# A hybrid decoder block on one core: another source for one Strassen-Winograd product, hand-fixed places for the input squares, and another order in the last value product

## The chip, the cores and the metric

The kernel runs on one core of a Trainium2 chip. The metric is the device time of one execution in microseconds; less is better. The engines of the core work side by side: TensorE (PE in the profile, its weight loads PEld), VectorE (DVE), ScalarE (ACT), GpSimd (POOL) and SyncE (SP), which issues the DMAs. Each engine takes its instructions in a fixed order.

## The reference

One block on x of 1024 tokens by 1024 channels, all in float32:

```python
xn = rmsnorm(h, norm_mix_g)
proj = xn @ w_in                                   # q, k, v (512 each), u, vg (512 each), 8 gates
log_f = log_sigmoid(proj[..., G_END:] + b_forget)
att = forgetting_attention(q, k, v, log_f)         # causal, 8 heads of 64, decay from cumsum(log_f)
u, vg = split(gelu(proj[..., V_END:G_END]))
sg = u * (tril(w_s) @ rmsnorm(vg) + b_s)           # in chunks of 128 tokens, 8 groups of 64
h = h + concat(att, sg) @ w_out
h = h + conv_ffn(rmsnorm(h, norm_ffn_g), ...)      # up 1024 -> 2*2816, causal conv of 3, silu gate, down
return rmsnorm(h, norm_final_g)
```

## The kernel before

**Products.** Every large product is a Strassen-Winograd product: the operands are cut in two by two blocks and seven products of blocks take the place of eight. Blocks of x transposed are `B11`, `B21` (first 512 tokens), and sums of blocks are `T1` to `T4` and `B22`, with the tokens' second half in them. Each operand is split into a rounded high part and a low part that is the rest; a block product is then three TensorE passes (high by high, high by low, low by high). ScalarE writes the high part (`act.copy`, or `activation` with the gain), VectorE the low part. `own` does so for one 128-row slice with the gain, `hl_of` for two slices whose gain is applied already, `tsplit` for a slice of weights, into a ring of six buffers. `tmul` issues the passes of one slice k for four token tiles, k by k: 12 matmuls, 48 for a product.

**Order.** A framework's scheduler puts each engine's instructions in order by its own estimates of when they are ready, earlier program text first among those that are. Two wrappers narrow this: while `act.on` and `dve.on` are true, every ScalarE and every VectorE call that goes through `act` and `dve` is tied behind the one before it on that engine; once they are false, later calls may be ordered freely, but each stays behind the last one of the hand-written stretch. Calls through `nc.scalar` are not bound, SyncE's and TensorE's neither. Because the wrappers make the calls, most ScalarE, VectorE and POOL rows show L51 (behind the previous one) or L44 (behind the floor) in place of the source line. Tiles with one tag share that tag's buffers, so a write can wait for the last reader of an older tile.

**First stage (0 to about 100 us).** The gating projections u and vg are made from seven products: B11, B21, then T2, T3, T1, T4 and B22; between B21 and T2 stand the low half of the values (`values_low`). The hand-written order covers this stretch up to T3's weights. The raw blocks of x sit in buffers that the split sets take over later: raw `x22` lies in tags x1, x2, where T3's split is to be written, and raw `x12` in tags t3, t2, where B22's is. `t2_of` has left a copy of x22 with its gain in `tmp[j][2]`. T3 = x12 g - x22 g is made in that copy. The squares of x for the first norm, one ScalarE instruction for each of 8 token tiles with `accum_out`, read `xq`, two halves in turn, so a load waits for the square two before; they stand as `nc.scalar`, outside the fixed order. `keep` evicts the kept low half of the values from PSUM and stores it to DRAM (`vd`). Behind the fixed stretch VectorE takes T2's result into `ut[1]`, adds weight blocks (`gb`), and makes T1's low parts.

**Keys and queries (about 100 to 188 us).** Four steps of products, with the forget gates in between: Exp, then Ln on ScalarE, each with a table load.

**Values and gating (188 to 224 us).** The second half of the heads' values comes from four products: T3 and B22 into four banks' halves `VH`, B11 and B21 into `VL`; two token tiles share a PSUM bank. `evac_v` evicts a tile: ScalarE's high part, VectorE's low part. `spatial` then goes through 8 groups, fixed order on: three matmuls into one of four banks, VectorE's product for the first half of the tokens, ScalarE's `second` for the other half, which GpSimd multiplies. The evictions of the value tiles 4 to 7 stand among the first groups, and a small Exp ahead of them loads the table that attention needs. `turn_sg` transposes the result for the output product, `sg_hi` and `sg_lo` split it, and attention's first logits take the PSUM banks over. Then follow attention (224 to about 500 us), the up products with the convolution, and the down products.

Of the kernel before, what the change touches and what calls it, by code (L numbers as in the profile page):

```python
# [65 lines left out]
def block_kernel(ctx: ExitStack, tc: tile.TileContext, xT, xtok, wuv, wv0, wv1, wqk, cpk, bfv,  # L66
# [37 lines left out]
    def f32(ap):  # L104
        return ap.bitcast(F32)
# [67 lines left out]
    def xset(tags):  # L173
        return [sb(t, [P, 2, 2, 512], F32R) for t in tags]
# [11 lines left out]
    def gk(k):  # L186
        return g1[:, k:k + 1]

    def xr(n, k):
        return RAW[n][k // 2][:, k % 2, :]  # L190
# [15 lines left out]
    def own(n, src, k, row):  # L206

        act.activation(xs(n, 0, k), src, AF.Copy, scale=gk(row))
        dve.scalar_tensor_tensor(out=xs(n, 1, k), in0=src, scalar=gk(row), in1=f32(xs(n, 0, k)),
                                 op0=ALU.mult, op1=ALU.subtract)  # L210

    def hl_of(n, j, src):
        act.copy(x2(n, 0, j), src)
        dve.tensor_tensor(out=x2(n, 1, j), in0=src, in1=f32(x2(n, 0, j)), op=ALU.subtract)
# [31 lines left out]
    def tsplit(src, gate=None, n=512, tag=None):  # L246
        w = sb(tag, [P, 2, n], F32R) if tag else ring(n=n)
        d = split_w(src, (w[:, 0], w[:, 1]))
        if gate:
            behind(d, gate)  # L250
        return w

    def tmul(banks, w, n, k, first, apart=False, ms_=range(4), own=True):

        ops = [(m, c) for m in ms_ for c in range(3)]
        for m, c in sorted(ops, key=lambda o: (o[1] > 0, o)) if apart else ops:
            ms = slice(m * P, (m + 1) * P)
            xi, wi = ((0, 0), (0, 1), (1, 0))[c]
            pe.matmul(banks[m], xs(n, xi, k)[:, ms], w[:, wi, :], start=(first and k == 0 and c == 0 and (own or m % 2 == 0)),  # L259
                      stop=(k == 3 and c == 2), skip_group_check=True)  # L260
# [30 lines left out]
    def keep(banks, hf):  # L291
        t = ring(F32).rearrange("p a (b c) -> p (a b) c", c=256)
        for m in range(4):
            act.copy(t[:, m, :], banks[m][:, 0:256])
            act.copy(zf[:, 4 * hf + m, 0:8], banks[m][:, 256:264])
        sp.dma_start(out=vd[hf], in_=t)
# [18 lines left out]
    values_low(3)  # L315

    xq = sb("A", [P, 2, 1024])
    for tt in range(8):
        t = xq[:, tt % 2, :]
        sp.dma_start(out=t, in_=xtok[tt * P:(tt + 1) * P, :])  # L320
        nc.scalar.activation(t, t, AF.Square, accum_out=ss1[:, tt:tt + 1])

    s2 = []

    def sum23(k):
        a11, a21, a22 = ua[k][:, 0, :], gb[k][:, 0, :], gb[k][:, 1, :]
        s2.append(sb("gg", [P, 512]))
        dve.tensor_tensor(out=a11, in0=a21, in1=a11, op=ALU.add)
        dve.tensor_tensor(out=s2[k], in0=a11, in1=a22, op=ALU.add)
# [4 lines left out]

    sum23(0)
    sum23(1)
    tmul(S, tsplit(s2[0]), "T2", 0, True)
    tmul(S, tsplit(s2[1]), "T2", 1, True)
    for k in (2, 3):
        sum4(k - 2)  # L340
        sum23(k)
    for k in (2, 3):
        tmul(S, tsplit(s2[k]), "T2", k, True)
    keep(B, 0)
    B, S = S, B
    for k in range(4):
        t3 = tmp[k // 2][2][:, k % 2]
        dve.scalar_tensor_tensor(out=t3, in0=xr("x12", k), scalar=gk(k), in1=t3, op0=ALU.mult, op1=ALU.subtract)
    XS["B22"] = xset(("t3", "t2"))
    for k in range(4):  # L350
        own("B22", xr("x22", k), k, 4 + k)
    XS["T3"] = xset(("x1", "x2"))
    for j in range(2):
        hl_of("T3", j, tmp[j][2])
        for k in (2 * j, 2 * j + 1):
            tmul(S, tsplit(ua[k][:, 0, :]), "T3", k, True)
    act.on = dve.on = False
    for m in range(4):
        dve.tensor_tensor(out=ut[1][:, m, :], in0=B[m], in1=vgt[0][:, m, :], op=ALU.subtract)
# [153 lines left out]
    def forget_sums(c, r):  # L513
        bfb, z, e = c[:, 136:144], c[:, 144:208], c[:, 208:272]
        tri, ones, lh, ll = r[:, 0:P], r[:, P:2 * P], r[:, 256:320], r[:, 320:384]
        v3 = lambda t: t.rearrange("p (h t) -> p h t", h=8)
        dve.tensor_tensor(out=v3(z), in0=zf[:, :, 0:8].rearrange("p t h -> p h t"),
                          in1=rstd1.unsqueeze(1).to_broadcast((P, 8, 8)), op=ALU.mult)
        dve.tensor_tensor(out=v3(z), in0=v3(z), in1=bfb.unsqueeze(2).to_broadcast((P, 8, 8)), op=ALU.add)
        dve.scalar_tensor_tensor(out=e, in0=z, scalar=-1.0, in1=z, op0=ALU.mult, op1=ALU.max)  # L520
        act.activation(e, e, AF.Exp, scale=-1.0)
        act.activation(e, e, AF.Ln, bias=one[:, 0:1])
        dve.tensor_scalar(out=z, in0=z, scalar1=-1.0, scalar2=0.0, op0=ALU.mult, op1=ALU.max)
        dve.tensor_tensor(out=z, in0=z, in1=e, op=ALU.add)
        dve.tensor_copy(lh, z)
        dve.tensor_tensor(out=ll, in0=z, in1=f32(lh), op=ALU.subtract)
        yield
        ps = bank()
        for o, m in ((64, tri), (128, ones)):
            pe.matmul(ps[:, o:o + 64], m, lh, start=True, stop=False)  # L530
            pe.matmul(ps[:, o:o + 64], m, ll, start=False, stop=True)
        whole, run = v3(ps[:, 128:192]), v3(e)
        dve.memset(run[:, :, 0:1], 0.0)
        for tt in range(1, 8):
            dve.tensor_tensor(out=run[:, :, tt:tt + 1], in0=run[:, :, tt - 1:tt], in1=whole[:, :, tt - 1:tt], op=ALU.add)
        dve.tensor_tensor(out=v3(z), in0=v3(ps[:, 64:128]), in1=run, op=ALU.add)

        yield
        pe.transpose(ps[0:64, 192:320], z, ident)
        rows = c[0:64, 272:400]  # L540
        act.activation(rows, ps[0:64, 192:320], AF.Copy, scale=-1.0)
        sp.dma_start(out=ncr.rearrange("h (t p) -> (h t) p", p=P), in_=rows)
        yield
# [118 lines left out]
    def evac_v(tt, hf, ps):  # L662
        v = V[tt // 2][:, tt % 2, 4 * hf:4 * hf + 4]
        p3 = ps.rearrange("p (h d) -> p h d", h=4)
        x = act.activation(v[:, :, 0, :], p3, AF.Copy, scale=rstd1[:, tt:tt + 1])
        dve.scalar_tensor_tensor(out=v[:, :, 1, :], in0=p3, scalar=rstd1[:, tt:tt + 1],
                                 in1=f32(v[:, :, 0, :]), op0=ALU.mult, op1=ALU.subtract)
        return x

    def kept(hf):  # L670
        t = sb("G" if hf else "wy", [P, 4, 256])
        sp.dma_start(out=t, in_=vd[hf])
        for j in range(4):
            if j % 2 == 0:
                V.append(sb("V", [P, 2, 8, 2, 64], F32R))
            x = evac_v(4 * hf + j, 0, t[:, j, :])
        return x

    kept(0)
# [38 lines left out]
    def spatial():  # L718

        act.on = dve.on = True  # L720
        after(tc, act.activation(pad[:, 0:1], eps, AF.Exp), stored)
        evac_v(4, 1, VH[0])
        tmp = [sb("pt", [P, 4, 256]) for _ in range(2)]
        for g in range(8):
            c, j = g // 2, g % 2
            ps = bank()
            pe.matmul(ps, ws[0][:, g, :], vgs[c][:, 0, j], start=True, stop=False)
            pe.matmul(ps, ws[0][:, g, :], vgs[c][:, 1, j], start=False, stop=False)
            m = pe.matmul(ps, ws[1][:, g, :], vgs[c][:, 0, j], start=False, stop=True)
            v3 = lambda t: t.rearrange("p (t d) -> p t d", d=64)  # L730
            u = [ut[hf][:, :, g * 64:(g + 1) * 64] for hf in range(2)]
            dve.scalar_tensor_tensor(out=u[0], in0=v3(ps[:, 0:256]), scalar=bs[:, g:g + 1], in1=u[0],
                                     op0=ALU.add, op1=ALU.mult)
            t = tmp[g // 4][:, g % 4, :]

            def second():
                act.activation(t, ps[:, 256:512], AF.Identity, bias=bs[:, g:g + 1])
                x = pool.tensor_tensor(out=u[1], in0=v3(t), in1=u[1], op=ALU.mult)
                after(tc, x, splits[0])

            if g < 7:
                second()
            if g < 3:
                evac_v(5 + g, 1, VH[1 + g])
        seq(m)
        return second

# [28 lines left out]
    S = [sbank() for _ in range(4)]  # L776

    def vbank(tt):
        return S[(2, 3, 0, 1)[tt // 2]][:, tt % 2 * 256:tt % 2 * 256 + 256]

    VH, VL = [vbank(4 + m) for m in range(4)], [vbank(m) for m in range(4)]
    a1 = [w0[k][:, :, 0:256] for k in range(4)]
# [28 lines left out]
    head_loads(0)  # L811
    for k in range(4):
        tmul(VL, w0[k][:, :, 256:512], "B21", k, False)
    stored = kept(1)
    ws = spatial_weights()
    for m in range(4):
        evac_v(m, 1, VL[m])
    for k in range(4):
        tmul(VH, tsplit(wvr[k][:, 1, :], n=256, tag="whl"), "B22", k, False)
    whs, wrs = [], sg_load(0)  # L820
    for s in range(2):
        after(tc, sp.dma_start(out=ncd[s].rearrange("h (t p) -> (h t) p", p=P), in_=sums[1 + s]), queued[0])
# [836 lines left out]
```

## Time and profile before

| | us |
|---|---|
| median of 3 runs | 1069.79 (1067.95 to 1070.84) |
| the profiled execution | 1069.69 |
| its span, first to last instruction | 1068.0 |
| TensorE busy | 1050.6 (98%) |
| VectorE busy | 887.0 (83%) |
| ScalarE busy | 571.9 (54%) |
| GpSimd busy | 236.5 (22%) |
| mean granted TensorE clock | 0.996 |

Busy time of TensorE is from modelled ends of pipelined matmuls, so a product that runs at half clock counts as busy too. In a timeline a row is: start in us, length in us, engine, line, operation, tiles out<-in, shape, count; then in brackets the engine's idle time ahead of it and what ended that. SPq is SyncE's DMA issue. In the waits' view a row is: who waited, for whom, us in total, times, longest.

### The profile page before, as it was taken

What the parts mean: (1) busy time and instruction counts of PE and PEld (TensorE: products, weight loads), DVE (VectorE), ACT (ScalarE), POOL (GpSimd) and SP (SyncE); (2) the same over time, 40 slices, a digit from 0 to 9 for tenths busy, and PEclk for the clock granted to TensorE, in tenths of its full rate; (3) what the DMA queues carried; (4) which work ended last, traced back from release to release, by engine and by line L of the source; (5) the groups of instructions that cost most, each with busy time, mean ns of one, the idle gap of its engine ahead of it and who ended that gap; (6) DMA issues with size and microseconds to landing.
All of it is one profiled execution on the core that took longest, in us unless ns stands there. A gap on an engine that the chain in (4) does not pass through costs nothing.

```text
span 1068.0 us, 14617 instructions
## 1 busy us (share of the span) xinstructions
PE 1050.6 (98%) x5156; PEld 882.5 (83%) x5156; DVE 887.0 (83%) x1299; ACT 571.9 (54%) x1015; POOL 236.5 (22%) x177
## 2 busy tenths in 40 slices
PE   9899999999999999999999999999999999999997
PEld 7778888978888887887888888888888888888886
DVE  6899697767777869999999989989998866997774
ACT  6677534466676846754444445444444444554653
POOL 0004141330420740053333333333322000000000
PEclk9999999999999999999999999999999999999999
DMA  9603365747555435132235423322321899433442
GB/s 338 199 12 129 100 170 157 226 122 209 169 156 163 136 143 204 60 99 95 102 129 173 152 88 110 108 94 94 123 105 62 294 321 318 118 99 94 144 121 96
DMA packets 67184, 155.78 MB, mean 146 GB/s; under 512 B 9028, under 2 KB 9748, under 8 KB 67112
## 3 DMA queue, kind: packets, MB, share of 16 engines
q1 hardware_dynamic: 65800, 154.82, 45.0%
q8 instruction: 40, 0.66, 0.3%
q14 instruction: 32, 0.26, 0.1%
q10 hardware_dynamic: 1312, 0.04, 0.1%
HBM read 111.96 MB, written 42.87 MB: 145 GB/s over the span
## 4 chain that ended last, share of the span: by engine, by line
PE 88%; DVE 5%; DMA 3%; ACT 2%; issue 1%; SPq 0%; DVEq 0%; ACTq 0%
PE k L1509 20%; PE qc L1251 11%; PE qa L1251 11%; PE qd L1251 10%; PE qb L1251 5%; PE ps L259 4%; PE pb L259 3%; PE pb L948 3%; PE pb L929 3%; PE qa L410 2%; PE qc L410 2%; PE qd L410 2%; PE pl L889 2%; PE pl L890 2%; PE pf L973 1%; PE pf L975 1%
## 5 line engine op out<-in xcount | busy, mean ns | idle before, releaser
L1509 PE MATMUL k<-whb,wha 128*128 128x512 f32 x924 | 209.7, 389 | 0.0
L1509 PEld LDWEIGHTS k<-whb,wha 128*128 128x128 f32 x924 | 173.3, 188 | 36.2 <-DVE wha L161 0.2
L1251 PE MATMUL qc<-xT,whb 128*128 128x512 f32 x540 | 130.0, 389 | 0.4 <-DVE u L1362 0.4
L1251 PE MATMUL qa<-xB,wha 128*128 128x512 f32 x528 | 127.3, 390 | 0.0
L1251 PEld LDWEIGHTS qc<-xT,whb 128*128 128x128 f32 x540 | 101.2, 188 | 22.1 <-DVE u L1362 0.9
L1251 PEld LDWEIGHTS qa<-xB,wha 128*128 128x128 f32 x528 | 98.8, 188 | 20.8 <-DVE wha L161 0.4
L155 ACT CAST wha<-sg 128x512 fp32r<-128x512 f32 x77 | 47.8, 622 | 96.9 <-PE k L1509 84.2
L155 ACT CAST whb<-sg 128x512 fp32r<-128x512 f32 x82 | 50.5, 618 | 86.7 <-PE qc L1251 68.3
L161 DVE TENSOR_TENSOR wha<-sg,wha 128x512 fp32r<-128x512 f32 x77 | 52.8, 688 | 40.5 <-ACT wha L155 40.4
L930 ACT CAST pt<-pb 128x512 fp32r<-128x512 f32 (+1 forms) x80 | 42.2, 544 | 43.0 <-PE pb L929 34.2
L1251 PE MATMUL qd<-xB,whb 128*128 128x512 f32 x264 | 63.9, 390 | 0.0
L1251 PE MATMUL qd<-xT,whb 128*128 128x512 f32 x264 | 63.6, 389 | 0.0
L161 DVE TENSOR_TENSOR whb<-sg,whb 128x512 fp32r<-128x512 f32 x82 | 57.7, 705 | 4.4 <-ACT whb L155 4.3
L1251 PE MATMUL qb<-xT,whb 128*128 128x512 f32 x252 | 60.9, 389 | 0.0
L1138 POOL TENSOR_TENSOR sg<-raw 128x512 f32<-128x512 f32 x20 | 30.4, 1518 | 136.1 <-DVE whb L161 75.7
L931 DVE TENSOR_TENSOR pt<-pb,pt 128x512 fp32r<-128x512 f32 (+1 forms) x80 | 48.8, 635 | 12.2 <-ACT pt L930 10.9
L1251 PEld LDWEIGHTS qd<-xB,whb 128*128 128x128 f32 x264 | 49.5, 188 | 10.7 <-DVE h L1370 0.5
L1251 PEld LDWEIGHTS qd<-xT,whb 128*128 128x128 f32 x264 | 49.5, 188 | 10.3
L1251 PEld LDWEIGHTS qb<-xT,whb 128*128 128x128 f32 x252 | 47.3, 188 | 9.8
L948 PE MATMUL pb<-pt,V 128*128 128x256 f32 x320 | 52.1, 287 | 0.3 <-DVE pt L931 0.2
L1141 POOL TENSOR_TENSOR sg<-sg,raw 128x512 f32<-128x512 f32 x20 | 33.3, 1666 | 64.2 <-DVE whb L161 64.2
L1139 POOL TENSOR_TENSOR sg<-sg,raw 128x512 f32<-128x512 f32 x20 | 34.9, 1746 | 50.7 <-issue 48.8
(404 smaller groups left out, 2292.5 us busy)
## 6 DMA issues: line engine op xcount, KB each, us to landing
raw<-wup SPq DMA_DIRECT2D x44, 512.0 KB
sg<-hx SPq DMA_DIRECT2D x77, 256.0 KB
hx<-hs SPq DMA_DIRECT2D x44, 256.0 KB
hx<-ca SPq DMA_DIRECT2D x35, 256.0 KB
xT<-wdn SPq DMA_DIRECT2D x28, 256.0 KB
x<-kd SPq DMA_DIRECT2D x24, 256.0 KB
A<-xtok SPq DMA_DIRECT2D x8, 512.0 KB
raw<-wqk SPq DMA_DIRECT2D x8, 512.0 KB
```

Source lines behind the costliest of these rows:

```text
L155: act.copy(h, src)
L161: return eng.tensor_tensor(out=l, in0=src, in1=f32(h), op=ALU.subtract)
L259: pe.matmul(banks[m], xs(n, xi, k)[:, ms], w[:, wi, :], start=(first and k == 0 and c == 0 and (own or m % 2 == 0)), stop=(k == 3 and c == ...
L410: pe.matmul(ps, w[:, wi, ks], xs(n, xi, k), start=(first and c == 0), stop=(c == 11), skip_group_check=True)
L929: seq(pe.transpose(ptr[:, c:c + P], tj[jj][:, k * P:(k + 1) * P], ident))
L930: casts.append(act.copy(pt[:, 0, 0:w], ptr[:, 0:w]))
L931: los.append(dve.tensor_tensor(out=pt[:, 1, 0:w], in0=ptr[:, 0:w], in1=f32(pt[:, 0, 0:w]), op=ALU.subtract))
L948: seq(pe.matmul(po[0][:, oo:oo + n], lhs, pt[:, s, o:o + n], start=(k == 0 and s == 0), stop=(s == 1 and half)))
L1139: pool.tensor_tensor(out=s[1], in0=s[0], in1=a11, op=ALU.add)
L1141: pool.tensor_tensor(out=s[3], in0=s[1], in1=a12, op=ALU.add)
L1251: pe.matmul(ps, w[:, wi, ks], xb[:, xi, k, :], start=(first and n == 0), stop=(n == 11), skip_group_check=True)
L1509: pe.matmul(banks[bk + m], xh[:, xi, ms], wh[:, wi, :], start=(first and p_ == 0 and n == 0), stop=(p_ == NP - 1 and n == 2), skip_group_c ...
```

## The change

Four things. T3's source is written over raw `x12` rather than over the copy of x22, T3's split comes right behind it, and B22 is split from the copy (two `hl_of` rather than four `own`) at the end of the hand-written stretch. The squares get places of their own in ScalarE's fixed order, among the weight casts. The last value product takes slices 0 and 1 for all tiles and then slices 2 and 3 tile by tile, with all its weight splits ahead; three of the four late evictions stand ahead of the gating's groups, the fourth's low part behind the first group; and the banks of the tiles are numbered in order. The small Exp moves behind the forget gates' Ln.

```diff
+    def squares(*tts):
+        for tt in tts:
+            t = xq[:, tt % 2, :]
+            sp.dma_start(out=t, in_=xtok[tt * P:(tt + 1) * P, :])
+            act.activation(t, t, AF.Square, accum_out=ss1[:, tt:tt + 1])
...
     sum23(0)
     sum23(1)
+    squares(0)
     tmul(S, tsplit(s2[0]), "T2", 0, True)
     tmul(S, tsplit(s2[1]), "T2", 1, True)
+    squares(1, 2)
     for k in (2, 3):
         sum4(k - 2)
         sum23(k)
     for k in (2, 3):
         tmul(S, tsplit(s2[k]), "T2", k, True)
+        squares(*((3,) if k == 2 else ()))
     keep(B, 0)
+    squares(4)
     B, S = S, B
     for k in range(4):
-        t3 = tmp[k // 2][2][:, k % 2]
-        dve.scalar_tensor_tensor(out=t3, in0=xr("x12", k), scalar=gk(k), in1=t3, op0=ALU.mult, op1=ALU.subtract)
-    XS["B22"] = xset(("t3", "t2"))
-    for k in range(4):
-        own("B22", xr("x22", k), k, 4 + k)
+        dve.scalar_tensor_tensor(out=xr("x12", k), in0=xr("x12", k), scalar=gk(k), in1=tmp[k // 2][2][:, k % 2],
+                                 op0=ALU.mult, op1=ALU.subtract)
     XS["T3"] = xset(("x1", "x2"))
     for j in range(2):
-        hl_of("T3", j, tmp[j][2])
+        hl_of("T3", j, RAW["x12"][j])
         for k in (2 * j, 2 * j + 1):
             tmul(S, tsplit(ua[k][:, 0, :]), "T3", k, True)
+        squares(5 + j)
+    squares(7)
+    XS["B22"] = xset(("t3", "t2"))
+    for j in range(2):
+        hl_of("B22", j, tmp[j][2])
     act.on = dve.on = False
...
-        act.activation(e, e, AF.Ln, bias=one[:, 0:1])
+        x = act.activation(e, e, AF.Ln, bias=one[:, 0:1])
+        after(tc, act.activation(pad[:, 0:1], eps, AF.Exp), x)
...
         act.on = dve.on = True
-        after(tc, act.activation(pad[:, 0:1], eps, AF.Exp), stored)
-        evac_v(4, 1, VH[0])
+        for m in range(3):
+            evac_v(4 + m, 1, VH[m])()
+        vlow = evac_v(7, 1, VH[3])
...
-            if g < 3:
-                evac_v(5 + g, 1, VH[1 + g])
+            if g == 0:
+                vlow()
...
-        return S[(2, 3, 0, 1)[tt // 2]][:, tt % 2 * 256:tt % 2 * 256 + 256]
+        return S[tt // 2][:, tt % 2 * 256:tt % 2 * 256 + 256]
...
-    for k in range(4):
-        tmul(VH, tsplit(wvr[k][:, 1, :], n=256, tag="whl"), "B22", k, False)
+    a12 = [tsplit(wvr[k][:, 1, :], n=256, tag="whl") for k in range(4)]
+    for k in range(2):
+        tmul(VH, a12[k], "B22", k, False)
+    for m in range(4):
+        for k in (2, 3):
+            tmul(VH, a12[k], "B22", k, False, ms_=(m,))
```

`evac_v` now returns its VectorE part as a function that the caller runs; elsewhere it is run at once.

More of the change, by code (lines that the diff above doesn't have):

```diff
@@ L317, in block_kernel @@
     xq = sb("A", [P, 2, 1024])
[L318 to L321, printed above, removed]
+    def squares(*tts):
[3 more added lines that the diff above has]
+            act.activation(t, t, AF.Square, accum_out=ss1[:, tt:tt + 1])
     s2 = []
@@ L665, in evac_v, with low @@
         x = act.activation(v[:, :, 0, :], p3, AF.Copy, scale=rstd1[:, tt:tt + 1])
-        dve.scalar_tensor_tensor(out=v[:, :, 1, :], in0=p3, scalar=rstd1[:, tt:tt + 1],
-                                 in1=f32(v[:, :, 0, :]), op0=ALU.mult, op1=ALU.subtract)
-        return x
+        def low():
+            dve.scalar_tensor_tensor(out=v[:, :, 1, :], in0=p3, scalar=rstd1[:, tt:tt + 1],
+                                     in1=f32(v[:, :, 0, :]), op0=ALU.mult, op1=ALU.subtract)
+            return x
+        return low
     def kept(hf):
@@ L675, in kept @@
                 V.append(sb("V", [P, 2, 8, 2, 64], F32R))
-            x = evac_v(4 * hf + j, 0, t[:, j, :])
+            x = evac_v(4 * hf + j, 0, t[:, j, :])()
         return x
@@ L813, in block_kernel @@
         tmul(VL, w0[k][:, :, 256:512], "B21", k, False)
-    stored = kept(1)
+    kept(1)
     ws = spatial_weights()
     for m in range(4):
-        evac_v(m, 1, VL[m])
-    for k in range(4):
-        tmul(VH, tsplit(wvr[k][:, 1, :], n=256, tag="whl"), "B22", k, False)
+        evac_v(m, 1, VL[m])()
+    a12 = [tsplit(wvr[k][:, 1, :], n=256, tag="whl") for k in range(4)]
[4 more added lines that the diff above has]
+            tmul(VH, a12[k], "B22", k, False, ms_=(m,))
     whs, wrs = [], sg_load(0)
```

## The prediction

> **What bounds the kernel now.** I read TensorE's waits over the whole span first, then the weight loads (PEld) in order of time around the two places that the waits name, then the windows with busy time and granted clock there, and last the timelines of ScalarE, VectorE and SyncE between them. TensorE's two longest waits inside the program lie in stages that the change touches:
>
> ```profile
> PE pb L259 <- ACT whl L51: 3.2, 1, 3.2
> PE pb L727 <- ACT pt L51: 1.6, 2, 0.8
> ```
>
> The first is the third product (T3) of the gating projections. Weight loads in order of time:
>
> ```profile
> 44.38 5.40 PEld L259 LDWEIGHTS ps<-wy,H 128*128 128x128 f32 x24
> 53.40 0.19 PEld L259 LDWEIGHTS pb<-whl,x 128*128 128x128 f32 x1 [3.63 <-ACT whl L51]
> ...
> 66.94 2.68 PEld L259 LDWEIGHTS ps<-wy,H 128*128 128x128 f32 x12
> ...
> 77.82 2.23 PEld L259 LDWEIGHTS pb<-whl,V 128*128 128x128 f32 x10
> ```
>
> T2 ends its loads at 44.38 + 5.40 = 49.78. T1, with 48 matmuls, runs without a gap from 66.94 to 77.82, 10.88 us or 0.2267 each. T3 also has 48, but takes 49.78 to 66.94, 17.16 us: 6.28 are lost. The windows say how (columns: length, busy time of PE, PEld, DVE, ACT, POOL with counts, granted clock, DMA):
>
> ```profile
> 50.20:53.40 3.20, 0.00 (x1) 0.00 (x0) 1.29 (x2) 3.20 (x6) 0.00 (x0) 1.00 0.19 78
> 55.30:58.70 3.40, 3.40 (x9) 2.65 (x8) 3.15 (x5) 3.40 (x7) 0.00 (x0) 0.50 0.00 0
> 215.70:219.10 3.40, 1.76 (x7) 0.84 (x6) 2.49 (x7) 1.56 (x4) 1.30 (x3) 1.00 0.97 223
> 219.10:222.50 3.40, 3.40 (x14) 3.01 (x14) 1.45 (x4) 1.92 (x6) 2.75 (x5) 0.50 0.44 158
> ```
>
> TensorE is idle for 3.20 us and, soon after, runs 3.4 us at clock 0.50. The same happens again after a window in which it was busy 1.76 of 3.40: a gap is paid for twice, once as idle time and up to 3.4/2 = 1.7 us more as slow matmuls behind it.
>
> The second place is the spatial gating, behind the last value product:
>
> ```profile
> 205.73 5.83 PEld L259 LDWEIGHTS ps<-whl,t 128*128 128x128 f32 x48
> 211.49 0.19 PEld L727 LDWEIGHTS pb<-H,wy 128*128 128x128 f32 x1
> 212.51 0.48 DVE L51 SCALAR_TENSOR_TENSOR A<-pb,cp,A 128x256 f32<-128x256 f32 x1 [0.42 <-PE pb L729]
> 213.03 0.47 ACT L51 ACTIVATE pt<-pb,cp 128x256 f32<-128x256 f32 x1 [1.46 <-DVE A L51]
> 214.30 0.47 DVE L51 SCALAR_TENSOR_TENSOR A<-pb,cp,A 128x256 f32<-128x256 f32 x1
> 219.77 0.23 PEld L753 LDWEIGHTS ps<-ident,A 128*128 128x128 f32 x1
> 222.98 0.91 PEld L753 LDWEIGHTS pb<-ident,A 128*128 128x128 f32 x8
> 223.10 1.89 DVE L51 TENSOR_TENSOR G<-ps,G 128x512 fp32r<-128x512 f32 x3 [0.45 <-ACT G L51]
> 224.44 0.19 PEld L889 LDWEIGHTS pl<-x 128*128 128x128 f32 x1 [0.56 <-DVE G L51]
> ```
>
> Eight groups of three matmuls need 24 x 0.2267 = 5.44 us, 211.49 to 216.93; the transposes start at 219.77, 2.84 late. One group takes 214.30 - 212.51 = 1.79 us, since VectorE, ScalarE's `second`, ScalarE's eviction and VectorE's low part of it follow each other, and from the fifth group on a bank must be freed so. Then come transposes at half clock, and attention's first logits at 224.44.
>
> **The change, T3.** In the old order T3's split waits for B22's four, since it is written over their source, and all of them share ScalarE with squares that wait for loads. The rows I build the new order from:
>
> ```profile
> 36.25 0.61 ACT L51 CAST whl<-gg 128x512 fp32r<-128x512 f32 x1
> 38.14 1.06 ACT L321 ACTIVATE A<-A 128x1024 f32<-128x1024 f32 x1 [1.29 <-DMA A<-xtok]
> ...
> 43.62 1.07 ACT L321 ACTIVATE A<-A 128x1024 f32<-128x1024 f32 x1 [0.64 <-DMA A<-xtok]
> ...
> 45.05 0.40 ACT L51 COPY whl<-pb 128x256 f32<-128x256 f32 x1
> ...
> 45.37 0.76 ACT L51 ACTIVATE t<-x,g 128x512 fp32r<-128x512 f32 x1
> ...
> 50.14 1.06 ACT L321 ACTIVATE A<-A 128x1024 f32<-128x1024 f32 x1 [1.55 <-DMA A<-xtok]
> ...
> 51.81 1.03 ACT L51 CAST x<-pt 128x1024 fp32r<-128x1024 f32 x1
> ```
>
> ```profile
> 39.32 0.33 SPq L320 DMA_DIRECT2D A<-xtok  x1
> ```
>
> ```profile
> 44.80 0.33 SPq L320 DMA_DIRECT2D A<-xtok  x1
> ```
>
> A square's load is issued when the square two before it is done, and it feeds ScalarE 43.62 - 39.32 = 4.3 us later (50.14 - 44.80 = 5.3 beside the store of `vd`). With fixed places, square 1 goes behind the cast of 36.25 and ends near 37.3; square 2 stays at 38.14; square 3's load, issued at 37.4, lands at 41.7, so square 3 ends at 42.8. Then the last T2 cast (to 43.3), eight copies of `keep` (four pairs at 45.37 - 45.05 = 0.32: 44.6), square 4 (45.7), T3's first cast, 1.03 (46.7), and two weight casts at 0.55 to 0.6 (47.8). VectorE:
>
> ```profile
> 43.02 1.41 DVE L51 SCALAR_TENSOR_TENSOR pt<-t,g,pt 128x512 f32<-128x512 f32 x2
> ...
> 52.87 1.23 DVE L51 TENSOR_TENSOR x<-pt,x 128x1024 fp32r<-128x1024 f32 x1 [0.18 <-ACT x L51]
> ...
> 54.01 0.68 DVE L51 TENSOR_TENSOR whl<-raw,whl 128x512 fp32r<-128x512 f32 x1
> ...
> 58.24 2.48 DVE L44 TENSOR_TENSOR A<-ps,G 128x512 f32<-128x512 f32 x4
> ...
> 65.81 0.65 DVE L44 TENSOR_TENSOR wy<-G,wy 128x512 fp32r<-128x512 f32 x1
> ```
>
> Its low part of the last T2 weights ends at 44.0, four in-place sums (0.7 each) end at 46.7, T3's low at 47.9, the first weights' low at 48.6. TensorE wants them at 49.78: 1.2 us to spare. The second half (cast behind square 5, low done near 51.8) is wanted 24 matmuls later, at 55.2. So T3 runs dense and ends at 49.78 + 10.88 = 60.66.
>
> What is late next is T1. B22's split now stands last in the hand-written order, behind square 7, and every later VectorE instruction is made to follow its second low part. Square 5 ends at 48.8 and square 7's load lands 3.7 to 5.3 later, at 52.5 to 54.2. Square 7, two casts of 1.03 and the last low of 1.23 put the end of the hand-written order at 56.6 (if no square waits for its load) to 58.8; I take 57.4, a load of 4.0, since by then only one other transfer is under way. Before, that point was 58.24. Behind it nothing of VectorE's work has changed: four `ut` differences, four weight sums, four T1 lows, the reciprocal, the first weights' low, 58.24 to 66.46, 8.22 us. So all of T1 but its first matmul starts at 57.4 + 8.3 = 65.7: TensorE waits 5 us there in place of 3.2 in T3. A window of low use again brings half clock: slow from the restart to the next window's edge, and one window more where the restart's own window was used less than half. Over the places where the edge can fall that costs 0.9 to 2.4 us, mean 1.6. T1 ends at 65.7 + 47 x 0.2267 + 1.6 = 77.9 against 77.82: **+0.1**, range -1.0 to +1.6. T3's 6.28 come back as a wait and slow matmuls one product later. From there TensorE has its old slack, its rows being dense to the value products.
>
> The window at 215.70 shows that half use is enough for the slow clock. The Trainium skill ("TensorE: Matmul & The Clock Gate", Part 1) says that the clock falls after one idle window of about 3.4 us; by that rule a 5 us gap holds a whole window only in some 45% of runs, the mean is 0.6 rather than 1.6, and the sum below would be 1.0 us less. The measured window speaks for the higher price.
>
> **The last value product and the gating.** Its 48 matmuls stay 5.76 us, 205.73 to 211.49. Tile by tile, the first bank (two tiles) is complete near 210.5, the second at 211.9. With hops of 213.03 - 212.51 = 0.52: the evictions of the first bank run from 210.5 to 212.4, the third tile's from 211.9 to 212.9, the first group's VectorE step at 212.9, `second` at 213.4, the fourth low behind it; the next groups follow at 0.4 to 0.5 rather than 1.79. The fifth group wants its bank at 214.2 and gets it at 213.9; the sixth 214.9 for 214.9. So the gating is dense: transposes at 216.93, no low window, full clock. The four sgT lows (the last three in the row of 223.10, 0.63 each) then set attention's start: four transposes and the cast behind them put the first low at 218.3, the second at 219.2, and the third is done at 220.5, against 224.4 before: **-3.85**. Bounds: -4.8 (TensorE alone: 24 transposes at 0.91/8 end at 219.65) and -2.0 (each of the four steps a hop late). The new bank numbers free the banks of the first transposes earlier; that costs nothing.
>
> **The table load.** It leaves this place and goes behind the keys' logarithm:
>
> ```profile
> 116.50 1.65 ACT L44 CAST whl<-raw 128x512 fp32r<-128x512 f32 x3
> 124.56 0.62 ACT L44 CAST G<-G 128x512 fp32r<-128x512 f32 x1 [6.41 <-DVE G L44]
> ...
> 209.17 1.28 ACT L51 ACT_TABLE_LOAD   x1
> ...
> 211.09 0.48 ACT L51 ACTIVATE V<-ps,rstd 128x256 fp32r<-128x256 f32 x1 [0.42 <-PE ps L259]
> ```
>
> At 209.17 it was hidden: ScalarE then still waited 0.42 for TensorE. At 116.5 it delays three casts by 1.5 us, in front of 6.4 us of idle time: 0. Without that cover it would cost 1.5.
>
> **Sum.** +0.1 - 3.85 = -3.75. The profiled execution took 1069.69 (span 1068.0, 1.69 around it), 0.1 under the median of 1069.79, so the forecast is **1065.9 us**. Its own ends are -1.0 - 4.8 = -5.8 and +1.6 - 2.0 = -0.4: 1063.9 to 1069.3. About 0.3%, 3.2 us, is what a measurement of this kernel can tell from no change.
>
> **The rivals.**
>
> *T1 is not held up* (10%). VectorE might do the `ut` differences and weight sums in its pause between 51.8 and 55. Its work from 44.0 on is 2.7 (sums) + 2.4 (T3) + 2.5 (weights) + 2.4 (B22) + 8.2 = 18.2 us, so T1 could start at 62.2 with no slow clock and end at 72.9: -4.9 - 3.85, 1060.9. Against it speaks the code: behind the hand-written order each call is tied to the last one in it.
>
> *The clock stays up behind a 5 us gap* (8%). If only a wholly idle window lowers it, T1's gap costs 1.0 less: 1064.9. This is the rule of the Trainium skill's page named above. The window that was busy 1.76 of 3.40 speaks against it.
>
> *Attention's start is held by a load* (10%). DMA was 0.97 busy at 215.70 to 219.10, and before, the first logits came only at 224.44. Had the first head's last load landed near there, the gating's 3.85 would turn into a DMA wait: 1069.69 + 0.1 = 1069.8. For it speaks the full DMA; against it, that the wait of 224.44 was for VectorE.
>
> *The squares block the split: slower* (10%). Square 4's load now stands behind the store of `vd` in the program. Rows of SyncE in the old order:
>
> ```profile
> 45.47 0.33 SPq L296 DMA_DIRECT2D vd<-whl  x1
> 47.38 0.33 SPq L320 DMA_DIRECT2D A<-xtok  x1
> ```
>
> There the store stands behind all eight loads in the program, yet goes out ahead of the last: the scheduler issues what it expects ready first, which is why I let square 4's load pass the store. If it doesn't, the load goes out at 45.1, lands 5.3 later at 50.4, and square 4, ahead of T3's first cast on ScalarE, ends at 51.5 rather than 45.7. T3's first weights are ready at 54.4 (4.7 us of idle TensorE), the order ends near 63.0, T1 at 63.0 + 8.3 + 10.65 + 1.6 = 83.5: +5.7 - 3.85 = +1.9, 1071.6. It decides from the point where the hand-written order ends later than about 61.
>
> **How the numbers follow.** The forecast has 62%. Two thirds of its spread lie below 1066.5, so it gives 0.42 to faster and 0.20 to the same. T1 free gives 0.10 to faster; the clock 0.07 and 0.01; the load 0.10 to the same; the squares, with 1.5 us either way, 0.05 to slower and 0.05 to the same. Together faster 0.59, same 0.36, slower 0.05. The range leaves out T1 free and the squares, 2 in 10, and holds the rest: 1063.0 (the forecast's low end and most of the clock's 1.0) to 1069.9 (the load).
>
> **What would show it.** Right: T3's weight loads without a gap behind T2's; one wait of about 5 us at the second matmul of T1, ended by VectorE's low part of the first weights; clock 0.50 right behind it; T4's first load within 1.5 us of 77.8. The last square near 53, VectorE's last step of the order near 57.4. Eight spatial groups at 0.69 each, no slow window there, first logits about 9.1 us behind the first spatial load (224.44 - 211.49 = 12.95 before). A third table load near 116.6 and none near 209. Wrong: a wait at T3 for ScalarE (the squares), T1 within 2 us of T3's end, or logits waiting for a DMA.

## The result and the profile after

| | before | after |
|---|---|---|
| median, us | 1069.79 (1067.95 to 1070.84) | 1064.06 (1063.68 to 1064.82) |
| ratio of the medians | 1 | 0.9951 (95%: 0.9937 to 0.9966) |
| profiled execution, us | 1069.69 | 1064.82 |
| its span, us | 1068.0 | 1063.1 |

The kernel is faster by 0.5%, 5.7 us by the medians and 4.9 by the profiled spans; 1065.9 was forecast, with a range of 1063.0 to 1069.9. TensorE's waits of the changed kernel, those of the two stages:

```profile
PE ps L259 <- DVE wy L44: 3.1, 1, 3.1
...
PE pl L907 <- DVE G L51: 0.7, 1, 0.7
```

T3's wait for ScalarE and the two for freed banks are gone. One wait for VectorE at T1 has come instead. The weight loads of the changed kernel in order of time, T3 to T4:

```profile
49.98 8.12 PEld L259 LDWEIGHTS pb<-whl,x 128*128 128x128 f32 x36
58.14 2.68 PEld L259 LDWEIGHTS pb<-wy,x 128*128 128x128 f32 x12
60.86 0.87 PEld L259 LDWEIGHTS ps<-wy,H 128*128 128x128 f32 x4
65.26 2.14 PEld L259 LDWEIGHTS ps<-wy,H 128*128 128x128 f32 x8 [3.53 <-DVE wy L44]
67.50 9.23 PEld L259 LDWEIGHTS ps<-whl,H 128*128 128x128 f32 x36
76.77 2.68 PEld L259 LDWEIGHTS pb<-whl,V 128*128 128x128 f32 x12
```

T3 is dense, 10.88 us. T1 issues four matmuls, waits 3.53, and its 36 later loads take 9.23 where T3's took 8.12. The windows with busy time and granted clock (length, busy time of PE, PEld, DVE, ACT, POOL, clock, DMA) show why:

```profile
62.99:66.40 3.41, 1.14 (x5) 0.95 (x6) 3.41 (x8) 1.94 (x4) 0.00 (x0) 1.00 0.14 1
66.40:69.81 3.41, 3.41 (x10) 2.65 (x9) 3.41 (x7) 3.30 (x6) 0.00 (x0) 0.50 0.00 0
69.81:73.22 3.41, 3.41 (x17) 2.80 (x16) 2.79 (x4) 2.23 (x3) 0.00 (x0) 1.00 0.00 0
```

VectorE, which holds T1, in the changed kernel's timeline:

```profile
54.73 1.23 DVE L51 TENSOR_TENSOR t<-pt,t 128x1024 fp32r<-128x1024 f32 x1 [3.10 <-ACT t L51]
55.87 1.22 DVE L51 TENSOR_TENSOR t<-G,t 128x1024 fp32r<-128x1024 f32 x1
57.01 2.48 DVE L44 TENSOR_TENSOR A<-ps,G 128x512 f32<-128x512 f32 x4
59.40 2.49 DVE L44 TENSOR_TENSOR G<-G 128x512 f32<-128x512 f32 x4
61.81 1.41 DVE L44 SCALAR_TENSOR_TENSOR H<-pt,g,H 128x512 fp32r<-128x512 f32 x2
...
64.57 0.64 DVE L44 TENSOR_TENSOR wy<-G,wy 128x512 fp32r<-128x512 f32 x1
```

Until 54.73 it is idle for 3.10 us, since B22's cast stands behind the last square on ScalarE. The gating in the changed kernel:

```profile
204.69 5.83 PEld L259 LDWEIGHTS ps<-whl,t 128*128 128x128 f32 x48
210.45 0.19 PEld L741 LDWEIGHTS pb<-H,wy 128*128 128x128 f32 x1
...
215.81 1.89 PEld L767 LDWEIGHTS ps<-ident,A 128*128 128x128 f32 x16
217.74 0.85 PEld L767 LDWEIGHTS pb<-ident,A 128*128 128x128 f32 x8
219.53 0.19 PEld L907 LDWEIGHTS pl<-x 128*128 128x128 f32 x1 [0.93 <-DVE G L51]
```

Eight groups take 215.81 - 210.45 = 5.36 us without a gap, and the logits follow 9.08 us behind the first group, where 12.95 were needed before.

The stretches between these stages run nearly the same code in all kernels, and but for waits behind T4 in experiments 3 and 6 they take the same time. So a profiled execution can be cut at the starts of a few weight loads, and the pieces add up to the span. Each number below is the difference of two such starts, in us (the value product is the last one; the last column tells T1's wait for VectorE's low part; "clock" is the mean granted clock of the profiled execution):

| kernel | start to T2 | T2 to T4 | T4 to value product | first group to logits | logits to end | clock | T1's wait |
|---|---|---|---|---|---|---|---|
| before | 39.04 | 38.78 | 127.91 | 12.95 | 843.56 | 0.996 | none |
| after | 39.20 | 37.57 | 127.92 | 9.08 | 843.57 | 0.997 | 3.53 |
| 1 gating alone | 39.29 | 37.24 | 127.91 | 9.08 | 843.32 | 0.997 | none |
| 2 T3 alone | 39.61 | 36.39 | 127.92 | 11.70 | 843.02 | 0.997 | 2.38 |
| 3 sums in the pause | 40.19 | 33.71 | 128.56 | 9.08 | 843.10 | 0.999 | 1.29 |
| 4 filled T1 gap | 39.47 | 35.81 | 127.93 | 9.07 | 842.46 | 0.999 | 0.24 |
| 5 before, filled | 39.21 | 38.21 | 127.93 | 12.31 | 842.78 | 0.999 | 1.00 |
| 6 B22 late too | 39.15 | 32.54 | 129.93 | 9.09 | 842.93 | 0.999 | none |
| 7 table load back | 39.39 | 35.25 | 127.92 | 9.12 | 843.36 | 0.998 | 2.79 |
| 8 value product by depth | 39.84 | 36.40 | 127.93 | 9.67 | 843.00 | 0.996 | 2.39 |
| 9 load behind store | 39.40 | 41.94 | 127.93 | 9.08 | 843.59 | 0.995 | 3.66 |
| 10 sums on GpSimd too | 39.33 | 32.53 | 127.92 | 9.08 | 843.18 | 0.999 | none |

The value product itself is 5.76 in all of them. From T2 to T4, 32.54 is the least: three products without a gap. The profiled 4.9 us of the change are 1.21 there and 3.87 at the gating, less 0.16 of a later start. Each row is one execution. The first stretch and the one from the logits to the end differ by up to 1.1 us between executions whatever the kernel, and from T2 to T4 the same old code took 38.78 before and 37.24 in experiment 1, the same new code 35.25 to 37.57 (the change, 2, 7 and 8). So the 1.21 of this one pair is uncertain by about its own size.

### The profile page after: what moved, and what is told of

The parts are those of the page before. It is cut to its first block, busy times and chain, and to the rows that moved or that the text cites. A ratio compares the mean times of both kernels' runs of the same rounds, so it can differ in the third digit from the quotient of the medians.

```text
span 1063.1 us, 14614 instructions
## 1 busy us (share of the span) xinstructions
PE 1048.1 (99%) x5156; PEld 881.9 (83%) x5156; DVE 886.9 (83%) x1297; ACT 571.2 (54%) x1013; POOL 234.5 (22%) x177
## 4 chain that ended last, share of the span: by engine, by line
PE 87%; DVE 7%; DMA 3%; ACT 2%; issue 1%; SPq 0%; DVEq 0%; ACTq 0%
PE k L1527 20%; PE qa L1269 11%; PE qc L1269 11%; PE qd L1269 10%; PE qb L1269 5%; PE ps L259 4%; PE pb L966 3%; PE pb L947 3%; PE pb L259 2%; PE qa L418 2%; PE qc L418 2%; PE qd L418 2%; PE pl L907 2%; PE pl L908 2%; PE pf L991 1%; PE pf L993 1%
```

## The experiments

Theory: VectorE's row of work behind the hand-written order holds T1, the gap makes the next window slow, and the gating's 3.9 us are real and independent of it. Rivals are named with each run. "Before" was run again on the same chip each time: 1069.83 us in the first four, 1068.88 in the next four, 1069.34 in the last two.

**1. The gating half alone** (before, with only the last value product, the evictions, the banks and the table load changed).

```diff
-        evac_v(4, 1, VH[0])
+        for m in range(3):
+            evac_v(4 + m, 1, VH[m])()
...
+    for m in range(4):
+        for k in (2, 3):
+            tmul(VH, a12[k], "B22", k, False, ms_=(m,))
```

> The kernel before with the last value product, the gating and the table load as changed; T3, B22 and the squares as before. Moved-wait theory: the gating gives its whole 3.9 us (first logits 9.1 us behind the first spatial load, no slow window there), time about 1065.6, ratio 0.9963. Rival (what the change gained came from T3, and attention's opening would have waited anyway): within 1 us of the kernel before, ratio 0.999 to 1.000.

Measured: 1065.86 us, ratio 0.9965 (0.9952 to 0.9977), 3.97 under before. The gating is as in the changed kernel to the hundredth (9.08).

**2. The T3 half alone** (before, with T3, B22 and the squares changed).

```diff
-        hl_of("T3", j, tmp[j][2])
+        hl_of("T3", j, RAW["x12"][j])
...
+        squares(5 + j)
+    squares(7)
```

> The kernel before with T3's source, B22's split and the squares as changed; the last value product, gating and table load as before. Moved-wait theory: T3 runs dense, T1 waits 3 to 5 us for VectorE and meets half clock, T4 begins 1 to 1.3 us earlier relative to T2 than before, so the time is 1.0 to 1.5 us less, ratio 0.9986 to 0.9990. Rival (T3's 6.3 us are gained): 4 to 6 us less, ratio 0.994 to 0.996.

Measured: 1066.09 us, ratio 0.9965 (0.9953 to 0.9978), 3.74 under before: not as expected. Two things made it, by the table. T2 to T4 gained 2.39 on the execution of before, since the last square's load landed earlier in this execution. The timelines of the second experiment and of the changed kernel:

```profile
51.86 1.06 ACT L51 ACTIVATE A<-A 128x1024 f32<-128x1024 f32 x1 [0.51 <-DMA A<-xtok]
```

```profile
52.61 1.06 ACT L51 ACTIVATE A<-A 128x1024 f32<-128x1024 f32 x1 [1.35 <-DMA A<-xtok]
```

Counted from T2's start that is 12.25 and 13.41 us, and T1's wait shrank with it. It stayed at 2.38, so the rival, by which all of T3's 6.3 us are gained, does not hold either. And the old gating, with all its waits, ran at full clock here. The slow windows of one execution begin whole multiples of 3.413 us apart (the last section has the figures); call these points its grid. Windows of the second experiment on its grid (64.70 plus multiples of 3.413):

```profile
211.46:214.87 3.41, 2.89 (x12) 1.75 (x10) 1.75 (x4) 1.52 (x5) 2.66 (x3) 1.00 0.75 184
214.87:218.28 3.41, 2.15 (x10) 1.50 (x11) 2.24 (x6) 2.40 (x6) 1.90 (x3) 1.00 1.02 252
218.28:221.69 3.41, 2.72 (x23) 2.32 (x21) 2.63 (x5) 3.12 (x7) 2.45 (x5) 1.00 0.19 68
```

And of the kernel before on its own grid:

```profile
215.61:219.02 3.41, 1.77 (x7) 0.81 (x7) 2.42 (x6) 1.52 (x5) 1.31 (x3) 1.00 0.96 220
219.02:222.43 3.41, 3.41 (x14) 3.02 (x15) 1.46 (x4) 1.98 (x5) 2.76 (x5) 0.51 0.46 163
```

The same waits fall into two windows of middling use in one case and fill half a window in the other; that is 12.95 - 11.70 = 1.25 us. So of the gating's 3.87, 2.62 is order and 1.25 is the clock. What moves the grid against the program is not known; it differs between executions.

**3. The four sums of `gb` in VectorE's pause.**

```diff
     squares(7)
+    for w in gb:
+        dve.tensor_tensor(out=w[:, 0, :], in0=w[:, 0, :], in1=w[:, 1, :], op=ALU.add)
     XS["B22"] = xset(("t3", "t2"))
...
-    for w in gb:
-        dve.tensor_tensor(out=w[:, 0, :], in0=w[:, 0, :], in1=w[:, 1, :], op=ALU.add)
```

> The changed kernel with the four weight sums (gb) moved into VectorE's pause of 3.1 us ahead of B22's low parts, in the fixed order. Moved-wait theory: VectorE is what holds T1, so T1's second round starts 2.4 us earlier, TensorE's wait there falls from 3.1 to under 1.2 us, the slow window goes away (1.5 us), and the time falls by 3.4 to 3.9 us against the changed kernel, to about 1060.4. Rival (T1 is held by ScalarE's weight casts or by the B bank's readers, VectorE only ends last): less than 1 us of gain, the wait stays near 3.

Measured: 1061.18 us, ratio 0.9917 (0.9904 to 0.9931), 2.9 under the changed kernel, by the ratios to before 3.6. That is a little less than expected: the wait stayed at 1.29, and 0.64 of the gain from T2 to T4 was lost again behind T4. No slow window but the one at the program's end. Its weight loads:

```profile
63.34 2.36 PEld L259 LDWEIGHTS ps<-wy,H 128*128 128x128 f32 x11 [1.29 <-DVE wy L44]
```

VectorE's queue holds T1: 2.5 us of its work moved ahead into a pause, with nothing else changed, shorten the wait and take the slow window away.

**4. Matmuls in T1's gap** (after, with 14 unused matmuls between T3 and T1, into banks that T1 starts afresh).

```diff
+    for n in range(14):
+        m = n % 4
+        t3mm2 = pe.matmul(B[m], xs("T3", 0, 3)[:, m * P:(m + 1) * P], xs("T3", 0, 2), start=True, stop=True, ...)
+        after(tc, t3mm2, t3mm)
+        t3mm = t3mm2
```

> The changed kernel with 14 extra matmuls (3.2 us) behind T3, into banks that T1 starts afresh; their results are not used. Nothing else moves: VectorE still holds T1. If the half clock behind the wait comes from the low use of the window ahead of it: no window at 0.50 near T1, time 1.3 to 1.7 us less than the changed kernel (about 1062.6). If the slow window has another cause: it stays, and the time is the same or up to 0.3 us more.

Measured: 1062.35 us, ratio 0.9929 (0.9916 to 0.9941), 1.7 under the changed kernel. The clock stays at 1.00 at T1, and its mean is 0.998 or 0.999 in all five executions, where the changed kernel had 0.996 or 0.997. So the low use of the window ahead is what halves it. From T2 to T4 it takes 1.76 less: the slow window's 1.65 are gone, VectorE's low came 0.80 earlier in this execution (64.73 - 39.47 = 25.26 behind T2's start, for 26.06), and one matmul instead of four stood ahead of the wait, which costs 0.68.

**5. Matmuls in the gaps of the kernel before** (14 between T2 and T3, 2, 4 and 4 behind the fifth to seventh group).

```diff
+    for n in range(14):
+        fm = pe.matmul(S[n % 4], xs("T2", 0, 3)[...], xs("T2", 0, 2), start=True, stop=True, ...)
...
+            for n in range({4: 2, 5: 4, 6: 4}.get(g, 0)):
+                fm = pe.matmul(S[2], ws[0][:, g, :], vgs[c][:, 0, j], start=True, stop=True, ...)
```

> The kernel before, with 14 unused matmuls between T2 and T3 and 2, 4 and 4 unused ones behind the fifth, sixth and seventh spatial groups, into banks that are started afresh afterwards. All waits stay as they are. Theory (the half clock is a cost of its own, and the kernel before pays it at two places at least; that is why each half of the change alone, -3.97 and -3.74, adds up to more than the whole, -5.7): the gaps are filled, the mean granted clock rises from 0.993-0.996 to 0.998-0.999, and the time falls by 1.65 at T3 and 1.25 at the gating, 2.9 in all, to 1066.9 (down to 1065.5 if executions with a lower mean clock had more than two slow windows). Rival (the T3 half gained by other loads landing earlier): the clock rises and the time stays within 1 us, 1068.8 to 1070.5.

Measured: 1067.31 us (11 runs), ratio 0.9986 (0.9977 to 0.9995), at a mean granted clock of 0.998 to 0.999. The gain of 1.5 lies between the two expectations; the table has 0.57 at T3 and 0.64 at the gating. At T3 a new wait took part of it:

```profile
55.09 7.80 PEld L259 LDWEIGHTS pb<-whl,x 128*128 128x128 f32 x35 [1.16 <-DVE whl L51]
...
66.84 2.38 PEld L259 LDWEIGHTS ps<-wy,H 128*128 128x128 f32 x11 [1.00 <-DVE wy L44]
```

T3's first low and T1's first low come when VectorE has them, so the slow window of the kernel before lay largely beside VectorE's work. At the gating the logits wait 1.52 for VectorE where the second experiment had 0.93; why is open. In the 39 executions of before that ran beside the ten experiments the time goes with the clock: 1070.1 us on average where its mean was 0.993 or 0.994 (12 of them), 1067.5 where it was 0.998 or 0.999 (4, from 1066.0 to 1069.3), some 0.55 us for 0.001. That is a correlation and no experiment. The two halves of the change gave 7.7 us in sum, the whole 5.7. Part of that surplus can lie in code that a half does not touch: against the traced execution of before, the second experiment's took 1.25 less at the old gating, at full clock, and the first's 1.54 less from T2 to T4. That this explains the medians is not shown.

**6. B22's split late** (the third, with B22's split behind T4 in the program and no longer in the hand-written order).

```diff
-    XS["B22"] = xset(("t3", "t2"))
-    for j in range(2):
-        hl_of("B22", j, tmp[j][2])
     act.on = dve.on = False
...
     tprod(S, lambda k: gb[k][:, 1, :], "T4", False)
+    XS["B22"] = xset(("t3", "t2"))
+    for j in range(2):
+        hl_of("B22", j, tmp[j][2])
```

> The third experiment (sums in the pause) with B22's split taken out of the hand-written order and put behind T4 in the program. Theory (the rest of T1's wait is VectorE's two B22 lows, 2.43 us, between the last T3 low and the ut differences): T1's first low, ready at 63.2 in the third experiment, comes 2.4 earlier, ahead of T3's end at 62.0; the waits of 1.3 + 0.5 go, 1.3 to 1.8 less than the third experiment's 1061.2: 1059.6. Rival (B22's split is then late for its own product, behind the activations on ScalarE): a wait of 1 to 2 us at B22 takes its place, 1061 to 1062.

Measured: 1061.14 us, ratio 0.9928 (0.9915 to 0.994): nothing over the third. From T2 to T4 it reaches 32.54, 1.17 better, and from T4 to the value product it loses 1.37:

```profile
104.41 1.39 PEld L259 LDWEIGHTS pb<-whl,x 128*128 128x128 f32 x11 [1.66 <-DVE whl L44]
```

The time lies in the rival's range, but not B22 waits, as the rival had it. The wait is at the value products behind B22 (264 columns wide, `values_high` in the kernel, just ahead of the keys' first products), 33 us after T4's start: VectorE's work up to there is the same in sum.

**7. The table load back at the gating** (after, with the small Exp ahead of the evictions again).

```diff
-        after(tc, act.activation(pad[:, 0:1], eps, AF.Exp), x)
...
         act.on = dve.on = True
+        after(tc, act.activation(pad[:, 0:1], eps, AF.Exp), stored)
```

> The changed kernel with the table load back at the spatial gating. Theory: it fits into ScalarE's wait of 1.23 us ahead of the first eviction and was hidden in the old order too: 0, 1064.1 (plus or minus 0.4). Rival: the evictions start a table load of 1.28 later and all of the gating with them: 1065.3.

Measured: 1064.06 us (1062.49 to 1066.42), ratio 0.9953 (0.9939 to 0.9967), against 0.9951 for the change: nothing. The load ran in ScalarE's wait:

```profile
206.00 1.28 ACT L51 ACT_TABLE_LOAD   x1
207.29 0.20 ACT L51 ACTIVATE pad<-eps 128x1 f32<-128x1 f32 x1
207.40 0.46 ACT L51 ACTIVATE V<-ps,rstd 128x256 fp32r<-128x256 f32 x1
```

**8. The last value product by depth** (after, with the old order k by k).

```diff
-    for k in range(2):
-        tmul(VH, a12[k], "B22", k, False)
-    for m in range(4):
-        for k in (2, 3):
-            tmul(VH, a12[k], "B22", k, False, ms_=(m,))
+    for k in range(4):
+        tmul(VH, a12[k], "B22", k, False)
```

> The changed kernel with the last value product in the old order, depth by depth for all four tiles, and all else of the change kept (four evictions ahead of the first spatial step, bank numbers, table load). Theory (the gating's gain is that the spatial steps no longer alternate with evictions; the tile order only frees the first bank some 0.7 us earlier): 0.3 to 0.8 more, 1064.4 to 1064.9, the gating still without a gap of over 0.5. Rival (the tile order carries the gain): 2 us or more, 1066 and up, with waits for freed banks in the gating.

Measured: 1064.28 us, ratio 0.9953 (0.9939 to 0.9966). By the trace 9.67 - 9.08 = 0.59 more at the gating, with gaps of 0.36 and 0.49. The median is only 0.2 above the changed kernel's, less than the runs can tell. Of the 2.62 the tile order carries 0.6; the remaining 2.0 are left for the evictions that no longer alternate with the groups' steps and for what goes with them (the low parts' places, the banks); these were not taken apart.

**9. The fifth square's load behind the store** (after, with square 4's load tied behind the store of `vd`).

```diff
-    keep(B, 0)
-    squares(4)
+    vst = keep(B, 0)
+    squares(4, behind_=vst)
```

> The changed kernel with the fifth square's load (square 4) made to follow the store of vd on its queue: the case in which the squares block the split. Theory (the prediction's own price): the load goes out near 44 to 45 in place of 41, lands 4.3 to 5.3 later, square 4 ends near 50 to 51 in place of 45.1, T3's first cast and its low part follow, and TensorE waits some 4 us for T3; the hand-written order ends 4 to 6 us later than 57.0 and T4 starts as much later: 4 to 6 us more, 1068 to 1070.5, slower than the changed kernel and about level with the kernel before. Rival (the loads and VectorE's slack hide it): under 2 us, up to 1066.

Measured: 1069.34 us (11 runs), ratio 0.9999 (0.999 to 1.0008): all of the change's gain is gone. ScalarE and TensorE of this kernel:

```profile
49.27 1.06 ACT L51 ACTIVATE A<-A 128x1024 f32<-128x1024 f32 x1 [5.38 <-DMA A<-xtok]
50.33 1.03 ACT L51 CAST x<-t 128x1024 fp32r<-128x1024 f32 x1
```

```profile
51.93 0.77 PEld L259 LDWEIGHTS pb<-whl,x 128*128 128x128 f32 x4 [1.79 <-ACT whl L51]
...
69.55 3.06 PEld L259 LDWEIGHTS ps<-wy,H 128*128 128x128 f32 x8 [3.66 <-DVE wy L44]
...
81.34 2.68 PEld L259 LDWEIGHTS pb<-whl,V 128*128 128x128 f32 x12
```

One load that goes out at 44.23, some 4.5 us later than the end of square 2 would allow, stands in ScalarE's fixed order ahead of T3's cast, and T4 comes 4.4 us later. The gating is untouched (9.08), and the clock is low for two windows in a row.

**10. Two more sums off VectorE** (the sixth, with `sum4(2)` and `sum4(3)` on GpSimd).

```diff
-        dve.tensor_tensor(out=a12, in0=s2[k], in1=a12, op=ALU.add)
+        (pool if k > 1 else dve).tensor_tensor(out=a12, in0=s2[k], in1=a12, op=ALU.add)
```

> The sixth experiment (sums in the pause, B22's split late) with two of VectorE's weight sums, 1.28 us together near 61.7, moved to the idle GpSimd. Theory (VectorE's row of work between 57 and 104 sets the start of the queries' products, where the sixth experiment waited 1.66 us for it; that is why the sixth gave nothing over the third): the wait falls to some 0.4, the time from 1061.1 to 1059.9. Rival (that wait hangs on ScalarE's activations, for which VectorE itself is idle 1.42 at 88.8): no change, 1061.1.

Measured: 1059.64 us (4 runs, 1059.28 to 1059.85), ratio 0.991 (0.9896 to 0.9923), the fastest of all, 9.7 under before on the same chip and some 4.4 under the changed kernel (by the ratios too). GpSimd needs 1.6 us for a sum that took VectorE 0.65, but does it in an idle stretch far ahead:

```profile
39.13 1.61 POOL L335 TENSOR_TENSOR raw<-gg,raw 128x512 f32<-128x512 f32 x1 [37.41 <-DVE gg L51]
42.15 1.62 POOL L335 TENSOR_TENSOR raw<-gg,raw 128x512 f32<-128x512 f32 x1 [1.41 <-ACT A L51]
```

```profile
60.98 2.68 PEld L259 LDWEIGHTS ps<-wy,H 128*128 128x128 f32 x12
63.70 8.12 PEld L259 LDWEIGHTS ps<-whl,H 128*128 128x128 f32 x36
...
102.44 1.52 PEld L259 LDWEIGHTS pb<-whl,x 128*128 128x128 f32 x12
```

No wait is left from T2 to the keys' products; the wait that went is the one at the value products (the expectation calls them the queries'). With the third and the sixth this shows VectorE's queue as the bound from T1 to these products.

## Why the prediction was right

The direction and the mechanism came out, and the size within the range, with one term mis-sized. The profiled sum is -4.9 for -3.75; the medians differ by 5.7, since the profiled execution of the changed kernel is the longest of its five.

**T3 dense: right.** Its loads run from 49.98 to 60.86, 10.88 us.

**The squares and the end of the hand-written order: right.** The squares' places, worked out from loads that land 4.3 us behind their issue, held to within 0.9 us; square 7's load landed at 52.6 and the order ended at 57.01, for 52.5 to 54.2 and 57.4 (56.6 to 58.8). The work behind it took 8.20 us up to the first weights' low, for 8.22.

**The wait at T1 and its end, +0.1 forecast, -1.21 measured: the mis-sized term.** The step said that T1 waits behind its *first* matmul, 47 left to do. The scheduler had put all four high-by-high matmuls of the first weights ahead; they need no low part. Only 44 matmuls were left, three fewer or 0.68 us. The restart, 65.26, was 0.44 earlier than 65.7, in an execution whose T2 lay 0.16 later. The slow window cost 1.5 for 1.6 (65.26 to 76.77 is 11.51 us, and 44 matmuls at 0.2267 are 9.97). Counted from T2 that makes -1.3 against the forecast, and the wait is 3.53 for 5. The order of the matmuls was counted from the program text, and the scheduler had chosen another; the row of T1 in the kernel before merges twelve loads and does not tell. How much of the -1.3 is this execution's luck with its loads is open: four executions of the new code took 35.25 to 37.57 from T2 to T4.

**The half clock.** It was right that a gap is paid for twice, and the fourth experiment shows the price, 1.65 us of its 1.76. But it is a matter of chance in each execution, which the prediction did not foresee: with the same T3 code three profiled executions had the slow window (the change, 2 and 8) and one had not (7), whose time of 1062.49 is the lowest of its five. Nor is half use always enough for the slow clock, as the prediction read from the window at 215.70: in the kernel before, an earlier window on the same grid, busy for 1.75 of 3.41 us, kept it:

```profile
48.45:51.86 3.41, 1.75 (x8) 1.13 (x6) 0.97 (x2) 1.86 (x5) 0.00 (x0) 1.00 0.68 274
51.86:55.27 3.41, 1.03 (x3) 0.67 (x4) 2.90 (x4) 3.41 (x7) 0.00 (x0) 1.00 0.01 4
55.27:58.68 3.41, 3.41 (x9) 2.65 (x9) 3.15 (x5) 3.41 (x7) 0.00 (x0) 0.50 0.00 0
```

The rule of the Trainium skill that was weighed ("TensorE: Matmul & The Clock Gate", Part 1: the clock falls after an idle window) does not describe these rows, in which windows busy for 1.03 to 1.77 of 3.41 us are followed by 0.50; what the same part says of a free-running grid agrees with slow windows at multiples of 3.413 us.

**The gating, -3.85 forecast, -3.87 measured: right**, down to the step (5.36 for 5.44 to the transposes, 9.08 for 9.1 to the logits). The prediction named the old kernel's slow window there, but did not price it: 1.25 of the 3.87 are that window, which is not there in every execution.

**The table load, 0: right, on both sides.** A third load stands among the forget gates at 115.56, and the casts behind it had 4.89 us of idle time where 6.41 had been:

```profile
115.56 1.28 ACT L44 ACT_TABLE_LOAD   x1
...
123.51 0.62 ACT L44 CAST G<-G 128x512 fp32r<-128x512 f32 x1 [4.89 <-DVE G L44]
```

The cast at 123.51 is 46.74 us behind T4's start, as it was before (124.56 - 77.82).

**The rivals.** "T1 is not held up" was excluded by the code, as argued: the order ties VectorE's later work behind B22's split. Its price was near, though: the third experiment, which moves four of those instructions ahead, came to 1061.18 where 1060.9 stood for the rival, and took 5.07 less than before from T2 to T4 where 4.9 had been worked out, with 1.29 of waiting left. "The clock stays up" is what some executions do. "Attention's start is held by a load" fell: the logits wait 0.93 for VectorE. "The squares block the split" did not happen, since square 4's load passed the store; forced in the ninth experiment it costs 5.3 us by the medians and 4.4 from T2 to T4 in the trace, where 5.7 (1071.6 less 1065.9) had been worked out. It takes the whole gain but does not make the kernel slower than before. The load went out at 44.2 and not 45.1, and the order ended at 61.3 and not 63.0.

## What to carry to other kernels

When a wait of TensorE is removed, follow the next engine's queue to the point where it is empty: here VectorE's work from T1 to the value products behind B22 was the bound, so of the 6.3 us lost at T3, 3.5 us came back as waiting and 1.5 as a slow window at T1, and only moving work into VectorE's pause or to an idle engine brought the rest. A fixed order makes one late load hold everything behind it, so what is placed in it should have its data long before. Read how many matmuls the scheduler really puts ahead of a wait, and compare kernels piece by piece between dense stretches: the median alone would have credited the T3 half with 3.7 us, though 1.25 of them lay at a gating that it does not touch.

## What the hardware showed

The slow windows of one execution lie on one grid of 3.413 us from the first stage to the end (55.3, 219.1 and 1065.6 in the kernel before, 48 and 248 steps), with another offset in each execution. A window followed by half clock had TensorE busy for 0.66 to 1.77 of its 3.41 us in eight cases (0.66, 1.03, 1.05, 1.14, 1.35, 1.45, 1.45, 1.77; by modelled ends); windows busy for 2.12, 2.15 and 2.38 were not. Nor were one of 1.44 us, at T1's gap in the seventh experiment, and one of 1.75, at 48.45 in the kernel before. So between some 40% and 60% the busy share alone does not tell which way it goes, and what else decides is not known. The slow window lasts one step where the next is well used, and two where it was itself used little (0.66 in the ninth).
